# Batch normalisation on one core: one tile's first columns loaded and another's stored in row groups

## The chip, the cores and the metric

The kernel runs on one core of a Trainium2 chip. The metric is the device time of one execution in microseconds (us). The kernel before takes 2485.12 us, the median of three runs (2484.46 to 2485.72).

A core has engines that work side by side: VectorE (DVE), ScalarE (ACT), GpSimd (POOL), TensorE (PE, not used here) and SyncE (SP), which here only issues transfers. Data lies in the chip's large memory (DRAM) or in the on-chip memory (SBUF), which has 128 partitions. Transfers between them (DMAs) are issued by an engine's queue and carried out by 16 DMA engines, each of which takes its share of a transfer's rows in turn. When an engine is done with its share of a DMA, it adds one to the DMA's semaphore; at sixteen the whole transfer has landed.

## The reference

Inference batch norm over an array of 32 images, 256 channels and 128 x 128 pixels, all in float32:

```python
eps = 1e-5
out = gamma * (x - mean) / np.sqrt(var + eps) + beta   # per channel
```

`x` and `out` have 537 MB each. `gamma`, `beta`, `mean` and `var` have one value for each of the 256 channels. With scale = gamma / sqrt(var + eps) and shift = beta - mean * scale, the work on each pixel is one multiplication and one addition.

## The kernel before, in words

The 256 channels are two blocks of 128, one channel to a partition, so the work is 64 tiles (32 images by two channel blocks) of 128 rows by 16384 columns: 64 KB a row, 8 MB a tile. A row is contiguous in DRAM and in its partition. Three buffers `t0`, `t1`, `t2` hold tiles in turn, and a tile is worked on in place: it is loaded, scaled and shifted, and stored from the same buffer. Ahead of the buffers lie the small tensors and a filler, `pad`, of 936 float32 a partition; with these sizes the first buffer starts at byte 28672 of each partition.

All DMAs are issued by SP (lines 83 to 91 and 151 to 161). At the start SP issues the left half of tile 0, the four parameter vectors (16 copies of each, into 16 rows of `rows`), the right half of tile 0, and tile 1. In the loop over the tiles `i` it waits until both engines are done with tile `i`, issues its store (L153), and then issues the load of tile `i + 2` (L158), which for `i > 0` first waits until the store of tile `i - 1` has landed, since it goes into the same buffer. So the queue holds store and load in turn, and the next transfer is in the queue before the one ahead of it has ended.

DVE turns the parameters into columns (L101 to L105) and computes `scale_t` and `shift_t` with one step on ACT (L107 to L117). Then DVE works on columns 0 to 9215 of every tile (`vector_part`, L123; tile 0 in two pieces) and ACT on columns 9216 to 16383 (`scalar_part`, L134). Every wait is written out by hand: `loaded`, `stored` and `early` count landings, `vdone` and `adone` the engines' parts, `vec` the steps of the setup. At the end SP waits for the last three stores (L165). POOL has nothing to do but four small memsets that the framework puts at the start (L180).

Of the kernel before, what the change touches and what calls it, by code (L numbers as in the profile page):

```python
# [8 lines left out]
NBUF = 3  # L9
PAD = 936  # L10
VMOST = 9216


@with_exitstack
def kernel(
    ctx: ExitStack,
    tc: tile.TileContext,
    x: bass.AP,
    gamma: bass.AP,
    beta: bass.AP,  # L20
    running_mean: bass.AP,
    running_var: bass.AP,
    out: bass.AP,
):
    nc = tc.nc
    eps = 1e-5
    f32 = mybir.dt.float32

    N, C, H, W = x.shape
    P = nc.NUM_PARTITIONS  # L30
    assert C % P == 0
    NCB = C // P
    HW = H * W
    NT = N * NCB
    B = 32
    NQ = P // B
    NE = 16
    NPAR = 4

    xr = x.rearrange("n (cb p) h w -> (n cb) p (h w)", p=P)  # L40
    outr = out.rearrange("n (cb p) h w -> (n cb) p (h w)", p=P)

    params = ctx.enter_context(tc.tile_pool(name="params", bufs=1))
    data = ctx.enter_context(tc.tile_pool(name="data", bufs=1))
    params.tile([P, PAD], f32, name="pad", tag="pad")
    bufs = [data.tile([P, HW], f32, name=f"t{s}", tag=f"t{s}") for s in range(NBUF)]
    rows = params.tile([B, NPAR * C], f32, name="rows", tag="rows")
    turned = params.tile([B, NPAR * C], f32, name="turned", tag="turned")
    par = params.tile([P, NPAR, NCB], f32, name="par", tag="par")
    eps_t = params.tile([P, 1], f32, name="eps_t", tag="eps")  # L50
    std_t = params.tile([P, NCB], f32, name="std_t", tag="std")
    rstd_t = params.tile([P, NCB], f32, name="rstd_t", tag="rstd")
    scale_t = params.tile([P, NCB], f32, name="scale_t", tag="scale")
    ms_t = params.tile([P, NCB], f32, name="ms_t", tag="ms")
    shift_t = params.tile([P, NCB], f32, name="shift_t", tag="shift")

    loaded = [tc.alloc_semaphore(f"loaded{s}") for s in range(NBUF)]
    stored = [tc.alloc_semaphore(f"stored{s}") for s in range(NBUF)]  # L60
    early = tc.alloc_semaphore("early")
    vdone = tc.alloc_semaphore("vdone")
    adone = tc.alloc_semaphore("adone")
    fetched = tc.alloc_semaphore("fetched")
    vec = tc.alloc_semaphore("vec")
    act = tc.alloc_semaphore("act")

    with tc.tile_critical():  # L68
        count = [0]

        def step(inst, sem=None, value=None):
            if sem is not None:
                inst._wait_ge(sem, value)
            elif count[0]:
                inst._wait_ge(vec, count[0])
            inst.then_inc(vec, 1)
            count[0] += 1
            return count[0]

        left, right = slice(0, HW // 2), slice(HW // 2, HW)  # L80


        nc.sync.dma_start(out=bufs[0][:, left], in_=xr[0][:, left]).then_inc(early, 16)
        zeroed = step(nc.vector.memset(rows[:], 0.0))  # L84
        for r, ap in enumerate((running_var, gamma, beta, running_mean)):
            inst = nc.sync.dma_start(out=rows[0:NE, r * C : (r + 1) * C], in_=ap.partition_broadcast(NE))  # L86
            if r == 0:
                inst._wait_ge(vec, zeroed)
            inst.then_inc(fetched, 16)
        nc.sync.dma_start(out=bufs[0][:, right], in_=xr[0][:, right]).then_inc(loaded[0], 16)  # L90
        nc.sync.dma_start(out=bufs[1][:], in_=xr[1]).then_inc(loaded[1], 16)

        def landed(i):
            return loaded[i % NBUF], 16 * (i // NBUF + 1)

        def gone(i):
            return stored[i % NBUF], 16 * (i // NBUF + 1)


        step(nc.vector.memset(eps_t[:], eps))  # L100
        step(nc.vector.transpose(out=turned[:], in_=rows[:]), fetched, 16 * NPAR)  # L101
        blocks = turned.rearrange("p (rc q b) -> p rc q b", q=NQ, b=B)
        flat = par.rearrange("p r cb -> p (r cb)")
        for q in range(NQ):
            placed = step(nc.vector.tensor_copy(out=flat[q * B : (q + 1) * B], in_=blocks[:, :, q, 0]))  # L105
        var_t, gamma_t, beta_t, mean_t = (par[:, r] for r in range(NPAR))
        nc.scalar.activation(  # L107
            out=std_t[:],
            in_=var_t,
            func=mybir.ActivationFunctionType.Sqrt,  # L110
            bias=eps_t[:],
            scale=1.0,
        )._wait_ge(vec, placed).then_inc(act, 1)
        step(nc.vector.reciprocal(out=rstd_t[:], in_=std_t[:]), act, 1)  # L114
        step(nc.vector.tensor_mul(out=scale_t[:], in0=gamma_t, in1=rstd_t[:]))  # L115
        step(nc.vector.tensor_mul(out=ms_t[:], in0=mean_t, in1=scale_t[:]))  # L116
        ready = step(nc.vector.tensor_sub(out=shift_t[:], in0=beta_t, in1=ms_t[:]))  # L117
        nc.vector.wait_ge(vec, ready)
        nc.scalar.wait_ge(vec, ready)

        def vector_part(i, first_col, end):
            t, cb = bufs[i % NBUF], i % NCB
            return nc.vector.tensor_scalar(  # L123
                out=t[:, first_col:end],
                in0=t[:, first_col:end],
                scalar1=scale_t[:, cb : cb + 1],
                scalar2=shift_t[:, cb : cb + 1],
                op0=mybir.AluOpType.mult,
                op1=mybir.AluOpType.add,
            ).then_inc(vdone, 1)  # L130

        def scalar_part(i, first_col, end=HW):
            t, cb = bufs[i % NBUF], i % NCB
            return nc.scalar.activation(  # L134
                out=t[:, first_col:end],
                in_=t[:, first_col:end],
                func=mybir.ActivationFunctionType.Identity,
                bias=shift_t[:, cb : cb + 1],
                scale=scale_t[:, cb : cb + 1],
            ).then_inc(adone, 1)  # L140


        vector_part(0, 0, HW // 2)._wait_ge(early, 16)
        vector_part(0, HW // 2, VMOST)._wait_ge(*landed(0))
        for i in range(1, NT):
            vector_part(i, 0, VMOST)._wait_ge(*landed(i))
        for i in range(NT):
            scalar_part(i, VMOST)._wait_ge(*landed(i))


        for i in range(NT):
            nc.sync.wait_ge(vdone, i + 2)
            nc.sync.dma_start(out=outr[i], in_=bufs[i % NBUF][:])._wait_ge(adone, i + 1).then_inc(  # L153
                stored[i % NBUF], 16
            )
            if i + 2 < NT:
                s = (i + 2) % NBUF
                inst = nc.sync.dma_start(out=bufs[s][:], in_=xr[i + 2])  # L158
                if i > 0:
                    inst._wait_ge(*gone(i - 1))  # L160
                inst.then_inc(loaded[s], 16)


        for i in range(NT - NBUF, NT):
            nc.sync.wait_ge(*gone(i))  # L165


# [28 lines left out]
```

## Time and profile before

| what | value |
| --- | --- |
| median of three runs | 2485.12 us |
| the profiled execution's own time | 2485.49 us |
| its span in the profile | 2483.7 us |
| DVE busy | 328.9 us (13%) |
| ACT busy | 408.7 us (16%) |
| POOL busy | 0.2 us |
| DMA queue of SP, share of 16 engines | 99.9% |
| data moved | 1073.84 MB, 432 GB/s over the span |
| DVE's part of a tile | 5.08 us |
| ACT's part of a tile | 6.36 us |

The span is the time from the first to the last instruction of the profiled execution; the execution's own time has 1.8 us more. DVE and ACT wait for loads nearly all the time. The chain of waits is, step by step, what released the next step; in it "another core or an unknown queue" stands for the time in which ACT waits for a load that was issued over 50 us earlier. So the start of ACT's part of a tile (line 134) tells when that tile has landed. GB/s is given for 40 equal slices of the span. A window's line has, after the window, its length, then for DVE, ACT and POOL the busy time and the number of instructions, then the clock, the share of the DMA engines' time that is busy and the rate. The trace also records single DMA packets (start, length, size) and single increments of the semaphores.

### The profile page before, as it was taken

To read this page: it belongs to the slowest core of one execution; us is meant where nothing else is said; L and a number is where in the kernel's file an instruction comes from. 1 tells how busy PE (TensorE), PEld (TensorE's weight loads), DVE (VectorE), ACT (ScalarE), POOL (GpSimd) and SP (SyncE) were. 2 spreads that over 40 slices of the span, in tenths; PEclk is the share of its full clock that TensorE was granted. 3 is DMA by queue.
4 is the path that set the end of the run, shared out by engine and by line. 5 is a ranking of instruction groups with operands and counts; after the bars stand their busy time and mean duration, and the time that the engine had idled before them with its cause. 6 is when DMAs were issued, how large, how long until landed. Compare 5 with 4: busy or idle time off the path is not lost.

```text
span 2483.7 us, 394 instructions
## 1 busy us (share of the span) xinstructions
DVE 328.9 (13%) x76; ACT 408.7 (16%) x66; POOL 0.2 (0%) x4
## 2 busy tenths in 40 slices
DVE  2111011110111101111011010110101101011010
ACT  2112121121211212112121121221212212112121
POOL 0000000000000000000000000000000000000000
DMA  9999999999999999999999999999999999999999
GB/s 410 436 433 431 433 436 432 433 436 436 429 436 436 433 433 436 437 430 435 437 432 433 436 437 430 436 436 431 434 437 435 431 436 437 431 434 437 435 429 397
DMA packets 18707, 1073.84 MB, mean 432 GB/s; under 512 B 2128, under 2 KB 2192, under 8 KB 2192
## 3 DMA queue, kind: packets, MB, share of 16 engines
q1 hardware_dynamic: 18704, 1073.82, 99.9%
q14 instruction: 3, 0.02, 0.0%
HBM read 536.94 MB, written 536.87 MB: 432 GB/s over the span
## 4 chain that ended last, share of the span: by engine, by line
another core or an unknown queue 81%; ACT 16%; DMA 2%; issue 0%; SPq 0%; DVE 0%; DVEq 0%
ACT t L134 16%; DMA t<-in_x_dram 2%; SPq L86 0%; DVE rows L84 0%; SPq L90 0%; DVE eps_t L100 0%; DVEq L191 0%; SPq L68 0%
## 5 line engine op out<-in xcount | busy, mean ns | idle before, releaser
L134 ACT ACTIVATE t<-t,shift_t,scale_t 128x7168 f32<-128x7168 f32 x64 | 407.1, 6361 | 2026.0 <-DMA t<-in_x_dram 2026.0
L123 DVE TENSOR_SCALAR t<-t,scale_t,shift_t 128x9216 f32<-128x9216 f32 (+1 forms) x65 | 325.4, 5006 | 2105.7 <-DMA t<-in_x_dram 2105.6
L101 DVE STREAM_TRANSPOSE turned<-rows 32x1024 f32<-32x1024 f32 x1 | 1.2, 1232 | 11.9 <-DMA rows<-in_running_mean_dram 11.9
L107 ACT ACTIVATE std_t<-par,eps_t 128x2 f32<-128x2 f32 x1 | 0.3, 295 | 14.0 <-DVE par L105 14.0
L107 ACT ACT_TABLE_LOAD x1 | 1.3, 1283 | 0.9 <-SPq L68 0.9
L84 DVE MEMSET rows<- 32x1024 f32 x1 | 0.9, 912 | 1.2 <-SPq L68 1.2
L105 DVE COPY par<-turned 32x8 f32<-32x8 f32 x4 | 0.6, 162 | 0.1
L114 DVE RECIPROCAL rstd_t<-std_t 128x2 f32<-128x2 f32 x1 | 0.2, 166 | 0.4 <-ACT std_t L107 0.4
L116 DVE TENSOR_TENSOR ms_t<-par,scale_t 128x2 f32<-128x2 f32 x1 | 0.2, 163 | 0.0
L115 DVE TENSOR_TENSOR scale_t<-par,rstd_t 128x2 f32<-128x2 f32 x1 | 0.2, 161 | 0.0
L117 DVE TENSOR_TENSOR shift_t<-par,ms_t 128x2 f32<-128x2 f32 x1 | 0.2, 160 | 0.0
L180 POOL MEMSET const-bfloat16-1.0<- 128x1 bf16 x1 | 0.1, 101 | 0.0
L180 POOL MEMSET const-uint8-127<- 128x1 uint8 x1 | 0.1, 101 | 0.0
L180 POOL MEMSET const-float32-0.0<- 128x1 f32 x1 | 0.1, 98 | 0.2 <-issue 0.2
L180 POOL MEMSET const-float32-1.0<- 128x1 f32 x1 | 0.1, 98 | 0.0
L100 DVE MEMSET eps_t<- 128x1 f32 x1 | 0.1, 59 | 0.1
## 6 DMA issues: line engine op xcount, KB each, us to landing
t<-in_x_dram SPq DMA_DIRECT2D x2, 4096.0 KB, 16.1
out_dram<-t SPq DMA_DIRECT2D x64, 51.6
t<-in_x_dram SPq DMA_DIRECT2D x63, 57.9
rows<-in_running_var_dram SPq DMA_DIRECT2D x1, 16.0 KB, 11.0
rows<-in_gamma_dram SPq DMA_DIRECT2D x1, 16.0 KB, 10.8
rows<-in_beta_dram SPq DMA_DIRECT2D x1, 16.0 KB, 10.6
rows<-in_running_mean_dram SPq DMA_DIRECT2D x1, 16.0 KB, 10.6
```

The source lines that it names most:

```text
L84: zeroed = step(nc.vector.memset(rows[:], 0.0))
L100: step(nc.vector.memset(eps_t[:], eps))
L101: step(nc.vector.transpose(out=turned[:], in_=rows[:]), fetched, 16 * NPAR)
L105: placed = step(nc.vector.tensor_copy(out=flat[q * B : (q + 1) * B], in_=blocks[:, :, q, 0]))
L107: nc.scalar.activation(out=std_t[:], in_=var_t, func=mybir.ActivationFunctionType.Sqrt, bias=eps_t[:], scale=1.0,)._wait_ge(vec, placed).t ...
L114: step(nc.vector.reciprocal(out=rstd_t[:], in_=std_t[:]), act, 1)
L115: step(nc.vector.tensor_mul(out=scale_t[:], in0=gamma_t, in1=rstd_t[:]))
L116: step(nc.vector.tensor_mul(out=ms_t[:], in0=mean_t, in1=scale_t[:]))
L117: ready = step(nc.vector.tensor_sub(out=shift_t[:], in0=beta_t, in1=ms_t[:]))
L123: return nc.vector.tensor_scalar(out=t[:, first_col:end], in0=t[:, first_col:end], scalar1=scale_t[:, cb : cb + 1], scalar2=shift_t[:, cb ...
L134: return nc.scalar.activation(out=t[:, first_col:end], in_=t[:, first_col:end], func=mybir.ActivationFunctionType.Identity, bias=shift_t[: ...
L180: nc = _bacc.Bacc("TRN2", target_bir_lowering=False, num_devices=1)
```

## The change

Tile 1's load and the last tile's (63's) store are cut up; everything else is moved as before.

- **Load of tile 1.** Columns 0 to 2047 (8 KB of each row) are loaded in six transfers of 24, 8, 8, 4, 4 and 80 rows, and then columns 2048 to 16383 of all rows in one. All are on SP's queue.
- **Store of tile 63.** Columns 2048 to 16383 go out in one transfer on SP's queue. Of columns 0 to 2047, rows 0 to 47 go out in five transfers of 24, 8, 8, 4 and 4 rows on POOL's queue, and rows 48 to 127 in one on SP's. Ahead of each of POOL's five stores POOL issues a short copy within SBUF, from columns 0 to 7 to columns 8 to 15 of a small new tensor `dummy`, of 4, 8, 8, 12 and 12 rows (32 bytes each). Its result is used by nothing.
- **`dummy`** is 16 by 16 float32, 64 bytes a partition; it is zeroed once by DVE. It lies ahead of the buffers, and `pad` is unchanged.
- **Waits.** The hand-written semaphores are gone. The work stands in `tc.manual_schedule()`, in which the framework keeps the written order on each engine and puts in the waits that the data needs. The order of a tile is now written as DVE's part, ACT's part, store, load of tile `i + 2`; on each queue this is the same order as before.

The core of the diff:

```diff
+PIECE = 2048
+GROUPS = (24, 8, 8, 4, 4)
+SHARES = ((24, 4), (8, 8), (8, 8), (4, 12), (4, 12))
...
+    dummy = params.tile([16, 16], f32, name="dummy", tag="dummy")
...
+    def load(i, rows=slice(0, P), cols=slice(0, HW)):
+        nc.sync.dma_start(out=bufs[i % NBUF][rows, cols], in_=xr[i][rows, cols])
+
+    def store(i, rows=slice(0, P), cols=slice(0, HW), queue=None):
+        (queue or nc.sync).dma_start(out=outr[i][rows, cols], in_=bufs[i % NBUF][rows, cols])
...
-    with tc.tile_critical():
+    with tc.manual_schedule():
+        load(0, cols=left)
...
-        nc.sync.dma_start(out=bufs[1][:], in_=xr[1]).then_inc(loaded[1], 16)
+        load(0, cols=right)
+        cut, first = slice(0, PIECE), 0
+        for n in GROUPS:
+            load(1, slice(first, first + n), cut)
+            first += n
+        load(1, slice(first, P), cut)
+        load(1, cols=slice(PIECE, HW))
...
+        nc.vector.memset(dummy[:], 0.0)
...
         for i in range(NT):
-            nc.sync.wait_ge(vdone, i + 2)
-            nc.sync.dma_start(out=outr[i], in_=bufs[i % NBUF][:])._wait_ge(adone, i + 1).then_inc(
-                stored[i % NBUF], 16
-            )
+            if i == 0:
+                apply_vector(i, 0, HW // 2)
+                apply_vector(i, HW // 2, VMOST)
+            else:
+                apply_vector(i, 0, VMOST)
+            apply_scalar(i, VMOST, HW)
+            if i < NT - 1:
+                store(i)
+            else:
+                store(i, cols=slice(PIECE, HW))
+                first = 0
+                for n, skip in SHARES:
+                    if skip:
+                        nc.gpsimd.dma_start(out=dummy[0:skip, 8:16], in_=dummy[0:skip, 0:8])
+                    store(i, slice(first, first + n), cut, nc.gpsimd)
+                    first += n
+                store(i, slice(first, P), cut)
             if i + 2 < NT:
-                s = (i + 2) % NBUF
-                inst = nc.sync.dma_start(out=bufs[s][:], in_=xr[i + 2])
-                if i > 0:
-                    inst._wait_ge(*gone(i - 1))
-                inst.then_inc(loaded[s], 16)
+                load(i + 2)
...
-        for i in range(NT - NBUF, NT):
-            nc.sync.wait_ge(*gone(i))
```

More of the change, by code (lines that the diff above doesn't have):

```diff
@@ L54 @@
     ms_t = params.tile([P, NCB], f32, name="ms_t", tag="ms")
+    dummy = params.tile([16, 16], f32, name="dummy", tag="dummy")
     shift_t = params.tile([P, NCB], f32, name="shift_t", tag="shift")
[L59 to L64, printed above, removed]
@@ L65 @@
-    vec = tc.alloc_semaphore("vec")
-    act = tc.alloc_semaphore("act")
-    with tc.tile_critical():
[L69 to L84, printed above, removed]
-        for r, ap in enumerate((running_var, gamma, beta, running_mean)):
[L86 to L90, printed above, removed]
-        nc.sync.dma_start(out=bufs[1][:], in_=xr[1]).then_inc(loaded[1], 16)
[L93 to L101, printed above, removed]
@@ new lines, with apply_vector, apply_scalar @@
+    left, right = slice(0, HW // 2), slice(HW // 2, HW)
+    def apply_vector(i, first_col, end):
+        t, cb = bufs[i % NBUF], i % NCB
+        nc.vector.tensor_scalar(
+            out=t[:, first_col:end],
+            in0=t[:, first_col:end],
+            scalar1=scale_t[:, cb : cb + 1],
+            scalar2=shift_t[:, cb : cb + 1],
+            op0=mybir.AluOpType.mult,
+            op1=mybir.AluOpType.add,
+        )
+    def apply_scalar(i, first_col, end):
+        t, cb = bufs[i % NBUF], i % NCB
+        nc.scalar.activation(
+            out=t[:, first_col:end],
+            in_=t[:, first_col:end],
+            func=mybir.ActivationFunctionType.Identity,
+            bias=shift_t[:, cb : cb + 1],
+            scale=scale_t[:, cb : cb + 1],
+        )
@@ new lines, in load @@
+    def load(i, rows=slice(0, P), cols=slice(0, HW)):
[4 more added lines that the diff above has]
+        load(0, cols=left)
+        nc.vector.memset(rows[:], 0.0)
+        for r, ap in enumerate((running_var, gamma, beta, running_mean)):
+            nc.sync.dma_start(out=rows[0:NE, r * C : (r + 1) * C], in_=ap.partition_broadcast(NE))
+        load(0, cols=right)
[5 more added lines that the diff above has]
+        load(1, cols=slice(PIECE, HW))
+        nc.vector.memset(eps_t[:], eps)
+        nc.vector.memset(dummy[:], 0.0)
+        nc.vector.transpose(out=turned[:], in_=rows[:])
@@ L104 @@
         for q in range(NQ):
-            placed = step(nc.vector.tensor_copy(out=flat[q * B : (q + 1) * B], in_=blocks[:, :, q, 0]))
+            nc.vector.tensor_copy(out=flat[q * B : (q + 1) * B], in_=blocks[:, :, q, 0])
         var_t, gamma_t, beta_t, mean_t = (par[:, r] for r in range(NPAR))
@@ L112 @@
             scale=1.0,
[L113 to L144, printed above, removed]
@@ L145 @@
-        for i in range(1, NT):
-            vector_part(i, 0, VMOST)._wait_ge(*landed(i))
-        for i in range(NT):
-            scalar_part(i, VMOST)._wait_ge(*landed(i))
-        for i in range(NT):
-            nc.sync.wait_ge(vdone, i + 2)
-            nc.sync.dma_start(out=outr[i], in_=bufs[i % NBUF][:])._wait_ge(adone, i + 1).then_inc(
-                stored[i % NBUF], 16
-            )
-            if i + 2 < NT:
-                s = (i + 2) % NBUF
-                inst = nc.sync.dma_start(out=bufs[s][:], in_=xr[i + 2])
-                if i > 0:
-                    inst._wait_ge(*gone(i - 1))
-                inst.then_inc(loaded[s], 16)
@@ L164 @@
-        for i in range(NT - NBUF, NT):
-            nc.sync.wait_ge(*gone(i))
+        )
+        nc.vector.reciprocal(out=rstd_t[:], in_=std_t[:])
+        nc.vector.tensor_mul(out=scale_t[:], in0=gamma_t, in1=rstd_t[:])
+        nc.vector.tensor_mul(out=ms_t[:], in0=mean_t, in1=scale_t[:])
+        nc.vector.tensor_sub(out=shift_t[:], in0=beta_t, in1=ms_t[:])
+        for i in range(NT):
+            if i == 0:
[15 more added lines that the diff above has]
+                store(i, slice(first, P), cut)
+            if i + 2 < NT:
+                load(i + 2)
```

## The prediction

> **What bounds the kernel now.** I read the page's parts 1 to 3 first (who is busy), then the answer by windows, then the chain of waits in order of time, then SP's own waits, and last the trace's records of single DMA packets.
>
> The page's first lines, its slices of DMA (busy tenths, and GB/s in 40 slices of 62.1 us) and its queues:
>
> ```profile
> span 2483.7 us, 394 instructions
> DVE 328.9 (13%) x76; ACT 408.7 (16%) x66; POOL 0.2 (0%) x4
> ...
> GB/s 410 436 433 431 433 436 432 433 436 436 429 436 436 433 433 436 437 430 435 437 432 433 436 437 430 436 436 431 434 437 435 431 436 437 431 434 437 435 429 397
> DMA packets 18707, 1073.84 MB, mean 432 GB/s; under 512 B 2128, under 2 KB 2192, under 8 KB 2192
> q1 hardware_dynamic: 18704, 1073.82, 99.9%
> ```
>
> The compute engines are idle for five sixths of the time; one queue keeps the 16 DMA engines busy for 99.9% of the span. Only transfer time, and how evenly the engines finish, can move the end.
>
> By windows (start, length, DVE, ACT, POOL, clock, DMA share, GB/s):
>
> ```profile
> 43.70:82.70 39.00, 5.08 (x1) 6.36 (x1) 0.00 (x0) 1.00 1.00 430
> 82.70:433.10 350.40, 45.72 (x9) 57.25 (x9) 0.00 (x0) 1.00 1.00 433
> 433.10:2443.20 2010.10, 264.13 (x52) 330.76 (x52) 0.00 (x0) 1.00 1.00 434
> 2462.60:2483.70 21.10, 0.00 (x0) 0.00 (x0) 0.00 (x0) 1.00 0.75 323
> ```
>
> The first ten tiles run slower than the other 52 although the engines never idle, and the last store's window is filled to 0.75 only. The chain of waits tells when each tile's load landed, for ACT starts then:
>
> ```profile
> 43.74 6.36 ACT t L134
> ...
> 82.73 6.36 ACT t L134
> ...
> 277.74 6.36 ACT t L134
> ...
> 433.15 6.36 ACT t L134
> ...
> 2443.24 6.36 ACT t L134
> ```
>
> 52 tiles from 433.15 take 2010.09, or 38.65 each; the ten before take 389.41, which is 2.9 us more than ten times 38.65, and 2.1 us of that fall in the six tiles up to 277.74. The packet records say why. A 64 KB row takes 2.418 us on every engine, loads and stores alike, and 32 KB take 1.213, so a packet costs about 8 ns and 36.8 ns a KB. What goes above 2.418 is in the last packets of a load, when other engines have begun the store behind it: up to 0.81 us on one packet at tile 1, 0.1 to 0.3 us an engine and tile until about 320 us, next to nothing later. Meanwhile the 16 engines drift apart: their increments for one load are spread over 0.66 us at tile 1, 2.5 us at 277.7, 4.2 us at the end. The drift ends the slow-down, and is paid once: the first engine is through its last store at 2477.7, the last at 2481.9.
>
> SP's own waits hold the tail; L165 is its wait for the last stores:
>
> ```profile
> SPq L158 <- DMA out_dram<-t: 769.2, 61, 12.8
> SPq L165 <- DMA out_dram<-t: 32.0, 1, 32.0
> ```
>
> **The change part by part.** *Loads in six groups.* A 128-row transfer leaves 128 packets and 16 increments: eight rows an engine. 24, 8, 8, 4, 4 and 80 rows divide evenly over 12, 8, 8, 4, 4 and 16 engines, and I assume that a short transfer starts at the first engine. For columns 0 to 2047 of tile 1 (8 KB packets, 8 + 8 x 36.8 = 0.30 us) the first four engines then get 2+1+1+1+1+5 = 11 rows, the next four 9, then 7, the last four 5. So the first four run 6 x 0.30 = 1.8 us behind the last four from tile 1 on. SP issues six more DMAs at 0.45 us (its row after 4.42 us) = 2.7 us, done by about 7.6 us, while the right half of tile 0 keeps the rings filled until 22.5 us: free, with 15 us to spare. Were that cover gone, 2.7 us would be paid.
>
> *What the stagger is worth.* Spread at tile 1 becomes about 0.66 + 1.8 = 2.5 us, which the kernel before reached at 277.7, having lost 2.1 us. Ends: nothing gained (the slow-down goes by which engines meet, not by how far apart they are), or all 2.9 us and the 0.66 of the start, 3.6. I take 2.1, the row of equal spread.
>
> *Stores.* Columns 2048 to 16383 go out as one SP transfer. The first 48 rows of the cut go out from POOL; as the code adds up (4+12 engines, then 8+8, 8+8, 12+4, 12+4 = 16 each time), every short copy moves the position so that the store behind it falls on the last engines. They then send 5, 7, 9 and 11 rows: the reverse of the loads, 16 rows on each engine in all. Without this the 1.8 us would stand at the end; with it the four groups end level but for the drift that is left. That is counted in the 2.1.
>
> *More packets.* Rows cut in two: 8 ns x 16 = 0.13 us an engine. An increment's packet is 9 ns; 6 load, 1 SP store, 5 POOL stores and 5 copies more: 17 x 9 = 0.15. Together 0.3 us on the path.
>
> *POOL's queue.* It had no DMA before, so no row prices its issue. All five copies write the same piece of `dummy`, so a copy may be made to wait for the one before; the first needs nothing of tile 63, which leaves three such waits after the first two stores. Each is bounded by 0.45 (SP's issue) + 2.4 (one packet ahead in the ring) = 2.9 us below and by the parameter copies' 11.0 us from issue to landing above (they queued behind a 4 MB load). With ten issues of 0.45 that is 13 to 37.5 us, begun when DVE ends tile 63 (2443.24 + 5.08 = 2448.3). The queue before ended 33.6 us later, so 0 to 4 us late. These copies have at most one packet per engine ahead, which is nearer to the low end: I take 0. What is queued behind each wait is the next store of 4 to 8 rows, and only the end of the kernel waits for those. SP's last store (80 rows) is issued behind its main store at about 2450 and waits for nothing else.
>
> *Addresses.* The tiles ahead of the data buffers grow by 64 bytes (`dummy`), and the buffers move from byte 28672 of a partition, a multiple of 4096, to 28736, not a multiple of 256. The row for it: the parameter copies land in `rows`, 32 bytes past a multiple of 256, and their 1 KB packets take 46 ns, just what 8 + 36.8 gives. Bounds: 0, or one more fixed part per stored row, 8 ns x 512 = 4.1 us an engine. I take 0, but that row is a write; reads of SBUF have none. [...]
>
> *The last 80 rows.* Five 8 KB packets an engine, 1.5 us, in the count above already. That engines write each other's partitions has one row: the 16-row parameter copies, 46 ns on each of 16 engines, no slower. I take 0. [...]
>
> *Waits.* The semaphores written out by hand become the framework's; ring order stays store, load, store, load, with the next transfer queued some 13 us before it is needed (store 0 is issued at 30.2, tile 1 lands at 43.7). Engine work stays: 0, within 0.5 us either way.
>
> *Sum.* The profiled execution took 2485.49 us (its span and 1.8 around it), 0.4 above the median of the runs: 2485.49 - 2.1 + 0.3 = 2483.7, and against the median 2485.12 it is 2483.3, which I predict.
>
> **The rivals.**
> *All of the drift saved:* 2485.1 - 3.6 + 0.3 = 2481.8. For it: later tiles run at 38.65 with nothing lost. Against: four engines still march in step within each group.
> *Drift as before:* the end moves only by the new packets, 0.3 us, or by 1 with the waits' half us: 2485.4 to 2486.1. For it: the settled spread is 4.2 us, not 2.5; against: half of the loss came below 2 us.
> *The other side, POOL's chain ends last:* from 2448.3 us on it has until 2480.1 before it sets the end (the median less the 3.2 us that lie behind the last increment, less the 1.8 gained), so it decides once it lasts over 31.8 us: with 4.5 us of issues, from 9.1 us a wait. At 11 us a wait (37.5) the time is 2448.3 + 37.5 + 3.2 = 2489.0; if an issue costs 1.5 us as well in place of 0.45, 10.5 more, 2499.5. For it: the rings are full of 2.4 us packets at that time, and a copy may wait for one at each of its steps. Against: an engine with nothing else queued answers fast, and the rings empty at 2480.
> *Reads off the boundary:* half to all of the 4.1 us on the forecast, 2485.3 to 2487.4. For it: no row prices such a read; against: the 46 ns write. [...]
> *The change does not do what it says:* if POOL's stores fall on the first engines too, those send 11 + 11 = 22 rows and not 16, 6 x 0.30 = 1.8 us more: 2485.1, and up to 2487 if drift falls on the same engines. For it: no row shows how POOL's transfers are dealt; against: the code's sums to 16.
>
> **How the numbers follow.** Forecast (2482.4 to 2484.6) 0.42, all saved (2481 to 2482.4) 0.10, as before 0.20, POOL's chain 0.14, reads 0.07, wrong engines 0.07. Range 2481.4 to 2489.0: it leaves out a part of the best case and the upper half of POOL's. The likeliest case alone is 2482.4 to 2484.6. Five us (0.2%, about what a measurement of this kernel tells from no change) is more than the whole 4.2 us of drift, so faster by that gets 0.03; slower, over 2490, is the worse half of POOL's chain and a tenth of the rest: 0.09; within 0.88.
>
> **What would show it.** Tile 1 landing about 0.9 us later; the steps from tile 1 to 11 at 38.7 and not 38.94; tile 63 landing near 2442; the increments of the last transfers within some 2.5 us. A last POOL store that lands after SP's, stored rows of over 2.418 us, or the first steps at 39 again would prove me wrong, each at its own step.

## The result

The change makes the kernel slower by 0.27%: 2491.74 us median (2490.95 to 2492.80, nine runs) against 2485.16 for the kernel before on the same chip (2483.96 to 2485.72, nine runs). The ratio is 1.0027, with a 95% interval of 1.0018 to 1.0035. The forecast was 2483.3 with a range from 2481.4 to 2489.0; the result is outside.

The profiled execution of the changed kernel has a span of 2490.5 us, 6.8 more than before. First its page: span, GB/s in 40 slices of 62.3 us, and queues.

```profile
span 2490.5 us, 540 instructions
...
GB/s 397 432 432 437 432 428 436 433 437 433 426 438 437 431 434 434 434 433 438 431 437 433 435 436 433 432 435 438 432 436 432 436 436 433 433 435 437 434 433 369
...
q1 hardware_dynamic: 18980, 1073.42, 99.7%
q0 software_dynamic: 336, 0.40, 0.1%
```

The first slice has gone from 410 to 397 GB/s and the last from 397 to 369; the 38 between are about as they were. q0 is POOL's queue, with all of its ten transfers. The order of time shows when tiles 1 and 63 had landed (ACT's part starts then):

```profile
47.04 6.36 ACT L76 ACTIVATE t<-t,shift_t,scale_t 128x7168 f32<-128x7168 f32 x1 [16.81 <-DMA t<-in_x_dram]
...
2448.17 6.36 ACT L76 ACTIVATE t<-t,shift_t,scale_t 128x7168 f32<-128x7168 f32 x1 [32.28 <-DMA t<-in_x_dram]
```

Tile 1 lands 3.3 us later than before (47.04 against 43.74), tile 63 4.9 us later (2448.17 against 2443.24), and the last instruction comes 6.8 us later. So of the 6.8 us, 3.3 are there after the first two tiles, 1.6 come in the long middle, and 1.9 after tile 63. The middle and the end by windows (start and end, length, DVE, ACT, POOL, clock, DMA share, GB/s):

```profile
47.00:435.90 388.90, 50.79 (x10) 63.60 (x10) 0.00 (x0) 1.00 1.00 433
435.90:2448.10 2012.20, 264.14 (x52) 330.76 (x52) 0.00 (x0) 1.00 1.00 434
2448.10:2490.50 42.40, 5.08 (x1) 6.36 (x1) 4.60 (x9) 1.00 0.79 336
```

The ten tiles after tile 1 take 388.9 us, where they took 389.4: almost none of the 2.1 us that the stagger was to save. The 52 after them take 2.1 us more than before. The end is now on POOL in the chain of waits:

```profile
2453.56 0.51 POOL out_dram L88
2454.07 14.15 DMA dummy<-dummy
...
2468.49 9.69 DMA dummy<-dummy
...
2478.46 7.35 DMA dummy<-dummy
...
2486.09 0.52 POOL dummy L137
2486.61 0.51 POOLq L168
```

And POOL's own waits:

```profile
POOL out_dram L88 <- DVE t L65: 2450.7, 1, 2450.7
POOL dummy L137 <- DMA dummy<-dummy: 29.0, 3, 13.4
```

The third, fourth and fifth copy do each wait for the one before: 13.4, 8.9 and 6.6 us, 29.0 in all. An issue takes 0.52 us. POOL's last store is issued at 2486.60 and lands at 2489.3; SP's last store lands at 2487.75. It would be easy to stop here and to blame the copies. The runs say otherwise.

### The profile page after: what moved, and what is told of

Read it like the earlier page. It is cut to its first block, busy times and chain, and to the rows that moved or that the text cites. A ratio compares the mean times of both kernels' runs of the same rounds, so it can differ in the third digit from the quotient of the medians.

```text
span 2490.5 us, 540 instructions
## 1 busy us (share of the span) xinstructions
DVE 328.8 (13%) x77; ACT 408.7 (16%) x66; POOL 5.4 (0%) x14
## 4 chain that ended last, share of the span: by engine, by line
another core or an unknown queue 83%; DVE 13%; DMA 3%; issue 0%; DVEq 0%; SPq 0%; POOL 0%; POOLq 0%
DVE t L65 13%; DMA t<-in_x_dram 2%; DMA dummy<-dummy 1%; DVEq L65 0%; SPq L85 0%; POOL dummy L137 0%; POOLq L168 0%; POOL out_dram L88 0%
```

## The experiments

Four things came in at once: row groups in the load, row groups in the store with POOL and its copies, the framework's waits, and 64 bytes that move the buffers. Each run was measured together with the kernel before on the same chip; the sixteen runs used three chips, and the median of the kernel before was 2485.2 to 2485.4 on each. The ratio need not be that of the two medians; its interval is about 0.09% wide to either side. Where small differences matter, the trace's packet records are used as well: "excess" is the time of all 64 KB rows above 2.418 us, as a mean over the 16 engines. It is that of one execution, the profiled one, whose time can lie some us from the median of its kernel.

### One part at a time

**e1: the load undone**

```diff
-        for n in GROUPS:
-            load(1, slice(first, first + n), cut)
...
-        load(1, cols=slice(PIECE, HW))
+        load(1)
```

> Tile 1 is loaded in one transfer again; the last tile's store stays cut up, with POOL's five stores and five copies. Theory (the row groups cost some 3 us at the start and make the engines drift further apart; POOL's chain of copy waits ends last): tile 1 lands at 43.7 us, the engines' spread at tile 63 is about 4.2 us again, tile 63 lands at 2443.2, and POOL's chain still takes 35.7 us from DVE's end of that tile (2453.6 to 2489.3 in the changed kernel), so it ends at about 2484.0 and the time is near 2486.5. Rival (the framework's waits or the buffers' new address cost the 6.6 us): the time stays at 2491 to 2492.

Measured: 2489.85, ratio 1.0015 (1.0006 to 1.0025). Tile 1 lands at 43.1, so the start is repaired, but the time falls by 1.9 us and not by 5. Even in the profiled execution, the shortest of the ten (2487.77), tile 63 lands at 2444.8 and its spread is 5.9 us, where 2443.2 and 4.2 were expected.

**e2: the store undone**

```diff
-                store(i, cols=slice(PIECE, HW))
...
-                store(i, slice(first, P), cut)
+            store(i)
```

> The last tile is stored in one transfer on SP; tile 1 is still loaded in six row groups. Theory: tile 1 lands at 47.0 and tile 63 at 2448.2 as in the changed kernel, the spread at tile 63 is near 6.9 us, the last increment comes 38.7 us after tile 63 (as before the change), at 2486.9, and the time is about 2490.1; so the store's part is worth 1.6 us and the load's part the rest. Rival (POOL's chain is the whole loss): about 2486.

Measured: 2489.71, ratio 1.0016 (1.0007 to 1.0025), as the first theory had it; tile 1 lands at 46.95.

**e3: both undone.** Both edits above; what is left are the framework's waits and the 64 bytes of `dummy`.

> Neither tile is cut up; what is left of the change is the framework's waits and the 64 bytes of dummy that move the buffers off a multiple of 256 bytes. Theory: the time is that of before, 2485.2 within 0.7, and tile 1 lands at 43.7. Rival (waits or address): 1.2 to 4 us above before, with 64 KB rows that take more than 2.418 us.

Measured: 2487.55, ratio 1.0007 (0.9998 to 1.0017). With neither tile cut up, 2.4 us of the 6.6 are still there, and the excess is 4.5 us an engine where it was 2.5. The theory (2485.2 within 0.7) fell here: waits or address do cost. (The rival had 1.2 to 4 us; no run gives its 1.2.) From e3 upward the parts roughly add: e2 is 2.2 us above it (the load's groups), e1 2.3 us (the store's), the whole change 4.2.

### Waits or address

**e5** is e3 with `PAD = 920` (64 bytes less, so the buffers start at 28672 as before the change). **e6** is the kernel before with `PAD = 952` (64 bytes more). **e7** is the whole change with `PAD = 920`.

> Neither tile is cut up, as in the run that took 2487.6, but the filler is 64 bytes smaller, so that the buffers start at byte 28672 again as in the kernel before; the framework's waits stay. Address theory (the 64 bytes cost the 2.4 us that were left): 2485.2 within 0.5. Waits theory: 2487.5 again.

> The kernel before with a filler that is 64 bytes larger and nothing else: hand-written waits, buffers at byte 28736. Address theory: 2487.5, with more 64 KB rows above 2.418 us than before. Waits theory: 2485.2.

> The whole change with a filler that is 64 bytes smaller (buffers at 28672). Address theory: 2.4 us less than the changed kernel, 2489.3, with tile 1 at 47.0 and POOL's chain ending last as before. Waits theory: 2491.7.

Measured: e5 2484.34 (ratio 0.9992, 0.9983 to 1.0001), e6 2487.22 (1.0004, 0.9995 to 1.0013; median 1.9 us above), e7 2489.28 (1.0012, 1.0003 to 1.0021). All three go with the address: taking the 64 bytes away is worth 3.2 us to e3 and 2.5 us to the whole change, adding them costs the old kernel 1.9. (e5 fell 0.9 us below the 2485.2 that the address theory gave it, beyond the 0.5 allowed.) Each step alone is near the edge of what its interval can tell; that three of three go the same way by a like amount is what carries it. No cost of the framework's waits shows; e5 is 1.0 us below the kernel before, which its interval does not tell from nothing.

Two more places, with the kernel before: **e12** with `PAD = 1000` (256 bytes more) and **e16** with `PAD = 968` (128 more).

> The kernel before with a filler that is 256 bytes larger, buffers at byte 28928, a multiple of 256 but not of 512 or 4096. If only the place within 256 bytes counts: 2485.3 as before, the last packets of loads above 2.418 us by 2.1 to 2.3 us an engine in all. If any move off 4096 counts: 2487.2, with 3.6 us or more.

> The kernel before with buffers at byte 28800, 128 bytes past a multiple of 256. At 64 bytes past it took 1.9 us more, at 256 nothing. If any place that is not a multiple of 256 costs: 2487 again; if only multiples of 64 that are not multiples of 128 do: 2485.4.

Measured: e12 2485.52 (ratio 1.0001, 0.9992 to 1.0010), e16 2487.82 (1.0012, 1.0003 to 1.0020). So 256 bytes cost nothing and 128 cost as much as 64 or more. By packet records, the excess of the kernel with hand-written waits, one execution each:

| buffers at | excess, us an engine | of it in the last packets of loads | median |
| --- | --- | --- | --- |
| 28672 (before) | 2.54 | 2.29 | 2485.2 |
| 28736 (e6, +64) | 5.17 | 4.76 | 2487.2 |
| 28800 (e16, +128) | 5.11 | 4.82 | 2487.8 |
| 28928 (e12, +256) | 2.66 | 2.27 | 2485.5 |

The cost is not in the stored rows. In e6 stores have 0.1 us of excess in all, and their median row is 2.418 us still. It is in the loads, where one engine's last packet of a load meets other engines' first packets of a store, the place where the kernel before loses its time too. More than half of it comes later in the run, though: after 330 us the excess is 3.0 us in e6 and in e16, and 0.6 in the kernel before. Why the places 64 and 128 bytes past a multiple of 256 make that meeting dearer is open. Nor is it the only thing that does: the profiled execution of e11 below, with buffers at 28672, took 2488.68 us, 3.5 above the median of its kernel, and has 6.3 us of excess. It is the medians that carry the address.

### What the load's groups cost

**e4: two halves.** Every engine gets eight rows; the last tile is stored whole (buffers at 28736).

```diff
-        for n in GROUPS:
-            load(1, slice(first, first + n), cut)
...
+        load(1, slice(0, P // 2), cut)
+        load(1, slice(P // 2, P), cut)
```

> Columns 0 to 2047 of tile 1 are loaded in two transfers of 64 rows (0 to 63, then 64 to 127), then the other columns; the last tile is stored whole. Each engine gets eight rows, as in the kernel before, so nothing is dealt unevenly; only which partitions are written at one time differs. Theory A (two engines that write partitions 0 to 63 share a way into SBUF): 8 KB packets take about 0.6 us in place of 0.31, tile 1 lands 2.4 us later than before, at 46.1, and the time is about 2487.6. Theory B (the uneven dealing of rows, or small packets as such, makes the loss): packets of 0.31 us with B's uneven dealing, tile 1 at 43.8 to 44 and the time 2485 to 2485.6; with small packets as such, 0.6 us packets here and also in a cut of 128 rows.

**e11: cut, but 128 rows together** (`load(1, cols=cut)`, and `store(i, cols=cut)` behind the main store; nothing on POOL; buffers at 28672).

> Columns 0 to 2047 of tile 1 are loaded, and of tile 63 stored, in one transfer of 128 rows on SP's queue; no row groups, nothing on POOL, buffers at 28672. Theory (the halves and groups were slow because of which partitions are written together): 8 KB packets of 0.31 us, tile 1 within 0.3 us of 43.0 and the time that of the uncut kernel at 28672, 2484.3, within 0.5. Rival (8 KB packets are slow as such while 16 engines move them): 0.6 us packets and 2 us more.

Measured: e4 2489.44 (1.0013, 1.0004 to 1.0023), 1.9 us above e3; e11 2485.20 (1.0001, 0.9992 to 1.0010; its profiled execution took 2488.68, so only its start is read here). The time of e11 is 0.9 us above e5, where 0.5 was allowed; tile 1 lands at 43.05, as expected. (e4's theory A had tile 1 at 46.1 and the time at 2487.6; tile 1 lands at 45.4, and the 64 bytes add what the theory left out.) The start of ACT's part of tile 1 in e3, e4 and e11:

```profile
43.23 6.36 ACT L76 ACTIVATE t<-t,shift_t,scale_t 128x7168 f32<-128x7168 f32 x1 [13.31 <-DMA t<-in_x_dram]
```

```profile
45.37 6.36 ACT L76 ACTIVATE t<-t,shift_t,scale_t 128x7168 f32<-128x7168 f32 x1 [15.00 <-DMA t<-in_x_dram]
```

```profile
43.05 6.36 ACT L76 ACTIVATE t<-t,shift_t,scale_t 128x7168 f32<-128x7168 f32 x1 [13.40 <-DMA t<-in_x_dram]
```

The window from 22 to 32 us, in which the cut columns go, in the kernel before, the changed one, e4 and e11:

```profile
22.00:32.00 10.00, 0.81 (x1) 6.36 (x1) 0.00 (x0) 1.00 0.99 429
```

```profile
22.00:32.00 10.00, 0.81 (x1) 6.36 (x1) 0.00 (x0) 1.00 1.07 311
```

```profile
22.00:32.00 10.00, 0.81 (x1) 6.36 (x1) 0.00 (x0) 1.00 1.07 346
```

```profile
22.00:32.00 10.00, 0.81 (x1) 6.36 (x1) 0.00 (x0) 1.00 1.10 472
```

The DMA engines count as busy throughout; what falls is the rate, from 429 GB/s to 311 and 346. (A packet is booked where it starts, which moves such a figure by some tens; e11 is not faster than the kernel before.) The packet records are plain: the cut's 8 KB packets take 0.309 us in e11, a median of 0.62 in e4, and up to 0.77 in the changed kernel's groups, whose first 56 KB packets take up to 3.9 us in place of 2.12 while other engines are still at their rows. So small packets are not dear by themselves, and the loss needs no uneven dealing. Rows 0 to 63 and rows 64 to 127, loaded apart, go at half the rate (0.62 us a packet against 0.309). Stores do not show it here: the 8 KB rows of the last 80 have a median of 0.309 us in the changed kernel, and so have all row groups of e14 below, though the engines come to them several us apart. The mean over the engines at which tile 1 is through is 42.6 us in e3, 44.6 in e4, 45.4 in e2 and in the changed kernel. Rows and partitions change together in e4, so whether the half rate comes from the partitions' side or from the other end of the transfer is not shown: the 0.6 us of theory A came (0.62), its shared way into SBUF is not shown.

### The store's part

**e8** is the whole change with a copy's columns apart (`dummy` 48 columns wide, copy `k` writes columns 8k+8 to 8k+15; `PAD = 904`, buffers at 28736). **e9** is the same at 28672 (`PAD = 888`). **e10** is e9 with each copy behind its store:

```diff
-                        nc.gpsimd.dma_start(out=dummy[0:skip, 8 * k + 8 : 8 * k + 16], in_=dummy[0:skip, 0:8])
                     store(i, slice(first, first + n), cut, nc.gpsimd)
+                    nc.gpsimd.dma_start(out=dummy[0:skip, 8 * k + 8 : 8 * k + 16], in_=dummy[0:skip, 0:8])
```

> The whole change, but each short copy writes eight columns of its own in a wider dummy, so none waits for the one ahead; the filler is smaller by as much, buffers at 28736 as in the changed kernel. If the copies' waits set the end: POOL issues all ten within about 6 us of DVE's end of tile 63, its stores land before 2475, SP's last store ends last, 1.5 us earlier than POOL did, and the time is near 2490.2. If POOL's transfers cost as such (their packets among the others): 2491.7 again.

> The whole change with buffers at byte 28672 and each short copy in columns of its own, ahead of its store: the kernel that the next run is compared with. Both theories: POOL no longer waits for copies, and the time is that of the whole change at 28672 (2489.3) or up to 1 us less. The engines that carry six of POOL's rows are those that end last, by 7 to 10 us behind the first.

> The same, but each copy is issued behind its store and not ahead of it, so that POOL's stores fall on the engines at the other end of the count. Theory A (in the change POOL's rows went to the engines that the loads had made late, 11 rows and 11 rows, and not to the early ones): the late engines now send 6 rows of 0.31 us less, 1.85 us, and the time falls to about 2487. Theory B (POOL's rows did go to the early engines as written, and the end is late for another reason): the time rises by 1 to 2 us, or stays within 0.5.

Measured: e8 2491.73 (1.0021, 1.0012 to 1.0029), e9 2489.31 (1.0016, 1.0007 to 1.0025), e10 2489.62 (1.0015, 1.0006 to 1.0024). POOL's waits in e9:

```profile
POOL out_dram L88 <- DVE t L65: 2447.5, 1, 2447.5
POOL out_dram L88 <- DMA out_dram<-t: 8.3, 1, 8.3
```

The three waits for copies (29.0 us) are gone, eight of the nine transfers that follow tile 63 are issued within 4 us, and the time is what it was: 2491.73 against 2491.74, 2489.31 against e7's 2489.28. The chain of waits named the copies truly as the last link, but SP's last store stood close behind (1.55 us in the changed kernel), and with POOL's rows issued earlier it lands later, at 2489.33 in e8 and not at 2487.75.

And the place of the copies makes no difference either. Theory A fell by the time: it expected 2487. B allowed for a time within 0.5 us, which is what came, but it has POOL's rows on the early engines, and the packet records show them on the late ones. In e9 the four engines with six of POOL's rows end at 2484.5 to 2486.3, and they were through tile 63 at 2443.4 to 2444.6; of those that end by 2478.9, the ones that can be followed have none, and were through tile 63 at 2440.9 to 2441.0. (Where two packets begin within a few ns of each other, their engines can't be told apart.) In e10, with every copy on the other side of its store, the engines with six rows that can be followed end at 2484.2 to 2486.0, and those with none by 2478.9. The late engines carry POOL's rows in both.

**e13** leaves the copies out (`PAD = 920`), all else as in the change.

> The whole change at 28672 without the five short copies. Theory A (the copies move nothing: POOL's stores start at the same first engines as SP's loads, with or without them, ahead or behind): 2489.3 within 0.5, and the engines that end last carry six of POOL's rows and were late at tile 63 already. Theory B (POOL's stores go on from engine to engine, and the copies move them): without copies the 24, 8, 8, 4 and 4 rows go round the engines, none carries more than four of POOL's rows, and the last engines end 0.6 us or more earlier.

Measured: 2488.89 (1.0014, 1.0005 to 1.0023), 0.4 below e7. The engines still carry six, four, two or none of POOL's rows, as five transfers do that start at the same engine each time; the last to end (2487.0) has six, and those with none that can be followed end at 2480.2 to 2481.0. Stores that went round the engines would have left none without rows. So the copies move nothing. And since the engines with six rows are late at tile 63 in all of these runs, and the late ones of tile 1 are those with eleven rows, POOL's rows start where SP's groups had started. (One engine's packets can't be followed from tile 1 to tile 63, so this last step is an inference.)

**e14: the store's groups on SP's queue**, tile 1 whole, no copies, 28672. **e15: three even groups of 16 rows on POOL's queue** (`SHARES = ((16, 0), (16, 0), (16, 0))`), tile 1 whole, no copies, 28672.

> Tile 1 loaded whole; the last tile's row groups (24, 8, 8, 4, 4, 80) are all stored on SP's queue, no copies, buffers at 28672. Theory A (the groups' rows pile up on the first engines whichever queue sends them): those send 11 rows and not 8, 0.9 us more, and rows that go out alone may share a way as the loads did: 2485.2 to 2486.5, against 2484.3 uncut. If it was POOL's queue that cost the 2 us of the store's part: 2484.3 to 2484.6.

> Tile 1 loaded whole; the first 48 rows of the last tile's cut go out on POOL's queue in three transfers of 16 rows, one row an engine each, no copies, buffers at 28672. If uneven dealing made the store's part dear: 2484.3 to 2485, all engines with three of POOL's rows. If POOL's queue as such did (its packets among the others): 2486 or more.

Measured: e14 2484.84 (1.0004, 0.9995 to 1.0013), e15 2485.76 (1.0001, 0.9992 to 1.0010), against e5's 2484.34. Both fall between what their two theories expected. Both lie within 1.5 us of the uncut kernel, and neither interval leaves 1. By the medians, piling the rows up costs little where the loads have not made the same engines late, and POOL's queue with even rows costs little too; but three of the eleven runs of e14 took 2489.8 to 2492.2, where none of the 33 of the kernel before beside them took over 2487.5, and no trace shows why. The 2.3 us of e1 over e3 were not found again in a single half of it. What part of them is POOL's copies (there POOL ends 1.9 us behind SP) and what part its rows among SP's packets was not settled. In the full change the copies are worth little: leaving them out (e13) takes off 0.4 us.

### The account

| part | runs | us |
| --- | --- | --- |
| buffers off 256 | whole change less e7 | +2.5 |
| load's row groups | e2 less e3 | +2.2 |
| store's groups, POOL and copies | e1 less e3 | +2.3 |
| the framework's waits (not clear of noise) | e5 less before | -1.0 |
| sum | | +6.0 |
| measured | | +6.6 |

e5, the change with neither tile cut up and the filler set right, is the fastest version of all, 2484.34 against 2485.37. Its interval (0.9983 to 1.0001) does not quite leave 1, so it is not claimed as a gain.

## Why the prediction was wrong

Three steps failed. The load's row groups were taken to move at full rate, and cost 2.2 us; the short copies were taken to steer POOL's stores to the early engines, and the store's part, which they were to make free, cost 2.3; the new address was taken at 0, and cost 2.5. Of the 2.1 us that were to be saved, little came. Two of the signs that the prediction named against itself came too: POOL's last store lands after SP's, and the ten steps after tile 1 are near 39 us again (38.9).

**What bounds the kernel** was right: the middle's engines are full (DMA share 1.00 from 47.00 to 2448.10 us), and what is won or lost is at the first tiles, the last one and in how far the engines drift apart.

**"What the stagger is worth", 2.1 us:** a part of it at best. The spread at tile 1 came out as forecast, near 2.5 us (2.1). At 28672 the excess is 2.36 us an engine without the groups (e5) and 1.33, 1.37, 1.07 and 1.86 with them (e7, e9, e10, e13). But 0.6 of the 2.36 falls at tile 1 itself, whose rows are cut in the other four and not counted (they lose more in another way); behind tile 1 it is 1.8 in e5, and 1.9 in e14 and 3.0 in e15, which load tile 1 whole too. At 28736 the excess behind tile 1 is 3.7 (e3) and 2.4 (e1) without the groups, 2.6 (the change), 2.8 (e8) and 2.9 (e2) with them. So a spread that is there from the start may save something at 28672, at most 0.7 us against e5, and nothing clear at 28736; single executions of a kernel differ by as much. Nor does the drift end with it: the spread at tile 63 is 6.9 us in the changed kernel (4.2 before), and 3.7 to 5.0 with the buffers at 28672. That the late engines of tile 1 stay late is likely, and not shown engine by engine.

**"I assume that a short transfer starts at the first engine", "free, with 15 us to spare":** the issuing was free, though with half of the room: SP waits 8.3 us for an earlier load on the way and is done at 15.1 us, not at 7.6.

```profile
SPq L85 <- DMA t<-in_x_dram: 8.3, 1, 8.3
```

The moving was not free. The step that failed is "The last 80 rows", taken at 0, and the groups' rows were not priced for the same thing at all. The row that it rested on, the parameter copies (1 KB rows, 46 ns on 16 engines), did not carry over to 8 KB rows; no run shows why. The tiles of the start cost 2.2 us in the time, 2.5 in the mean of tile 1. (Where nothing slows it an 8 KB row takes 0.309 us; the 0.30 of the forecast counts 8 KB as 8000 bytes, which changes little.)

**"Every short copy moves the position so that the store behind it falls on the last engines":** this is the step that carried the plan, and it fell. It was read from the code's sums, not from any row. With the copies ahead, behind or left out, the late engines carry six of POOL's rows; by the inference above they are those that the loads had made late, and send 11 + 11 rows. The rival for it was priced at 1.8 us over the forecast and given 0.07, a low chance for something that no row of the profile bore out.

**"POOL's queue", 13 to 37.5 us, taken at 0 late:** the chain lasted 35.7 us (2453.6 to 2489.3), near the upper end. The rival had it decide from 31.8 us on, and it is indeed the last link; but without it (e8, e9) the time stays. So its 0 was right by luck: the waits were nearly as long as the prediction's upper end, and the engines with POOL's rows end as late without them. No run shows the 1.5 us an issue of the rival's worst case; POOL's issues took 0.52 us in the changed kernel.

**"Addresses", 0 to 4.1 us, taken at 0:** 1.9 to 3.2 us in four comparisons at 64 bytes (before and e6, e5 and e3, e7 and the change, e9 and e8). Both the row (a write of 1 KB packets) and the bound (a dearer stored row) looked at single packets; the loss is in how loads and stores of different engines meet (4.76 of the 5.17 us of excess in e6 are in the last packets of loads).

**The waits,** within 0.5 us either way: e5 is 1.0 below the kernel before, not clear of noise.

The range to 2489.0 took each of these at its worst one at a time. Three came together.

## What to carry to other kernels

When a kernel runs its DMA engines full, cut its loads so that every piece still spans all 128 rows: a piece of 64 rows was loaded at half the rate here (8 KB packets of 0.62 us in e4 against 0.309 in e11), though the DMA engines counted as busy throughout (share 1.07 from 22 to 32 us). A short tensor that is put ahead of big buffers can move them: 64 bytes past a multiple of 256 cost this kernel 1.9 to 3.2 us and 128 bytes 2.6, while a move by 256 cost nothing (0.2, within the noise); look at where the buffers start after every such edit. And where a plan needs to know which engine gets which rows, test that alone and read it from the packet records: who carries which rows shows, in any run with such stores, that the copies move nothing.

## What was not expected of the hardware

- Buffers 64 or 128 bytes past a multiple of 256 went with twice the slow-down of loads where other engines begin their stores (excess of 5.2 and 5.1 us an engine against 2.5, one execution each), while single 64 KB rows kept 2.418 us in both directions elsewhere.
- A copy of 32 bytes a row from POOL took 7.4 to 14.2 us from its issue until the next could start, while the rings held SP's rows of 64, 56 and 8 KB.
- The link that a chain of waits shows last need not set the time: 29.0 us of waits on it were taken out (one wait of 8.3 us for an earlier store came in their place) and the time stayed the same.
